# The block-to-block step of an S5 scan by doubling instead of one block after the other

## The chip, the cores and the metric

The kernel runs on one core of one Trainium2 chip. The metric is the device time of one execution in microseconds, as the median of several runs. The chip's engines are named as in the profile: PE is TensorE (PEld its weight loads), DVE is VectorE, ACT is ScalarE, POOL is GpSimd and SP is SyncE, which only issues transfers here.

## What is computed

One inference step of a decoder trunk of two layers, for 1024 prompt rows and 8 x 8 sample rows that share the weights (1088 rows of 1024 features). Layer 0 has two mixers side by side behind one input projection: an S5 state space (32 groups of 16 channels, 64 complex states each) and a gated DeltaNet (GDN, 4 heads). Layer 1 is an RWKV-7 mixer. Each layer ends with a SwiGLU feed-forward part. The change is in S5. What matters of the reference there:

```python
bu = einsum("gpc,blgc->blgp", bb, uf)
bu[:, 0] += ab * h0
x[t] = ab * x[t - 1] + bu[t]
y = real(einsum("gcp,blgp->blgc", c, x)) + d_skip * uf
```

All of `ab`, `bu`, `x` and `c` are complex and are held as a real and an imaginary part; the recurrence runs over the 1024 prompt rows, and for the samples over 8 rows each.

## The kernel before, in words

**Rows, chunks, blocks.** S5 cuts time into chunks of 8 rows: 128 chunks for the prompt and one for each of the 8 sample sequences. Inside a chunk the work is matrix products; from chunk to chunk the state is carried by a scan. The tile `Z` (128 partitions x 2 x 16 x 136) holds, for 16 state columns, the real and the imaginary part of the state before each chunk. A chunk's step multiplies by `a` to the power 8, where `a` is `ab` above.

**Constants** (`S5.consts`, L580). Small VectorE instructions on 128x16 work out `a` and its powers: `pw` holds powers 0 to 8, `p8` (L671) holds the powers 0 to 8 of `a` to the 8th, each by a complex multiplication `cmul` (L650, six instructions). `p8s` (L681) is a copy of the imaginary parts, once with the sign turned. The planner places these among the work that prepares the input rows.

**Adding up** (`S5.adds`, L760). For each of four groups `m` of four state columns the input part of every chunk is computed on TensorE and copied into `Z`.

**The scan** (`S5.scan`, L786). It is called twice, once for groups 0 and 1 and once for groups 2 and 3, each time on 8 state columns. All of it is VectorE work. A step (L793 to L800) adds to a part `o` of `Z` a power times a part `x` of `Z`, as four instructions: two multiplications into `m1` and `m2`, their sum, and the addition to `o`. The 128 chunks stand as 16 blocks of 8. First each block is scanned by itself: 7 steps on all 16 blocks at once (256 columns, L802). Then the last chunk of each block is carried to the last chunk of the next one: 15 steps, each on one block (16 columns, L804). Then each block's carried state is added to the first seven chunks of the next one: 7 steps on 15 blocks (240 columns, L806), which do not depend on each other. GpSimd then copies the final state and the sample states, and a last step advances the samples.

**Outputs** (`S5.outputs`, L819). Per group, TensorE multiplies `Z` (L840) and the inputs (L838) by weights made in `weights` (L717), and ScalarE and VectorE apply a GELU (L842 to L845).

**The order of the work.** Behind S5 in the program stand the input projections of the GDN (`qkvz`, L1806, products `pi` of L322) and the GDN segments, whose tiles take the room that S5 leaves. The framework's planner orders the instructions of every engine's queue by a simulated time line (L2112); nothing in S5 fixes an order by hand. So the projections are spread among the S5 products on TensorE. Each queue is worked through in its order on the chip.

Of the kernel before, what the change touches and what calls it, by code (L numbers as in the profile page):

```python
# [8 lines left out]
F32 = mybir.dt.float32  # L9
# [559 lines left out]
class S5:  # L569
# [10 lines left out]
    def consts(self, after, lam_re, lam_im, log_step, b_re, b_im, c_re, c_im, dskip, h0):  # L580
        K, nc, cp = self.K, self.K.nc, self.cp
        v = nc.vector
# [3 lines left out]
        def col(name, n=16):  # L586
            return cp.tile([128, n], F32, name=name)
# [32 lines left out]
        z = col("zz")  # L620
# [29 lines left out]
        def cmul(o, a, b, e, tag):  # L650

            (orr, oi), (ar, ai), (br, bi), sh = o, a, b, list(o[0].shape)
            tl = lambda: (self.wp or cp).tile(sh, F32, tag=tag, name=tag)
            t = tl()
            e.tensor_mul(orr, ar, br)
            e.tensor_mul(t, ai, bi)
            e.tensor_sub(orr, orr, t)
            t = tl()
            e.tensor_mul(oi, ar, bi)
            e.tensor_mul(t, ai, br)  # L660
            e.tensor_add(oi, oi, t)
# [6 lines left out]
        b4 = lambda i: pw[:, i, 4:5, :].to_broadcast([128, 4, 16])  # L668
        cmul((pw[:, 0, 5:9], pw[:, 1, 5:9]), (pw[:, 0, 1:5], pw[:, 1, 1:5]), (b4(0), b4(1)), v, "cm4")

        p8 = cp.tile([128, 2, 9, 16], F32, name="p8")  # L671
        self.p8 = p8
        v.tensor_copy(p8[:, :, 0:1], pw[:, :, 0:1])
        v.tensor_copy(p8[:, :, 1:2], pw[:, :, 8:9])
        Q = lambda j: (p8[:, 0, j], p8[:, 1, j])
# [2 lines left out]
        cmul(Q(4), Q(2), Q(2), v, "cm")  # L678
        b8 = lambda i: p8[:, i, 4:5, :].to_broadcast([128, 4, 16])
        cmul((p8[:, 0, 5:9], p8[:, 1, 5:9]), (p8[:, 0, 1:5], p8[:, 1, 1:5]), (b8(0), b8(1)), v, "cm4")  # L680
        p8s = self.p8s = cp.tile([128, 2, 9, 16], F32, name="p8s")  # L681
        v.tensor_scalar(p8s[:, 0], p8[:, 1], -1.0, None, op0=OP.mult)
        v.tensor_copy(p8s[:, 1], p8[:, 1])

# [101 lines left out]
    def scan(self, fin, qs):  # L786

        nc, wp, Z, SV = self.K.nc, self.wp, self.Z, self.SV
        v = nc.vector
        nq = qs.stop - qs.start  # L790
        z = Z[:, :, qs, 1:129].rearrange("p i q (b j) -> p i q b j", j=8)

        def step(o, x, j, n):  # L793

            m1 = wp.tile([128, 2, nq, 16], F32, tag="m1", name="m1")[:, :, :, :n]
            m2 = wp.tile([128, 2, nq, 16], F32, tag="m2", name="m2")[:, :, :, :n]
            v.tensor_mul(m1, x, self.p8[:, 0, j, qs][:, None, :, None].to_broadcast([128, 2, nq, n]))
            v.tensor_mul(m2, x[:, 1::-1], self.p8s[:, :, j, qs][:, :, :, None].to_broadcast([128, 2, nq, n]))
            v.tensor_add(m1, m1, m2)
            v.tensor_add(o, o, m1)  # L800

        for j in range(1, 8):  # L802
            step(z[:, :, :, :, j], z[:, :, :, :, j - 1], 1, 16)
        for b in range(1, 16):  # L804
            step(z[:, :, :, b:b + 1, 7], z[:, :, :, b - 1:b, 7], 8, 1)
        for j in range(7):  # L806
            step(z[:, :, :, 1:16, j], z[:, :, :, 0:15, 7], j + 1, 15)

        nc.gpsimd.tensor_copy(fin[:, :, qs, 0:1], Z[:, :, qs, 128:129])
        nc.gpsimd.tensor_copy(Z[:, :, qs, 128:136], self.h0[:, :, qs])  # L810
        step(SV[:, :, qs], Z[:, :, qs, 128:136], 1, 8)
        nc.gpsimd.tensor_copy(fin[:, :, qs, 1:9], SV[:, :, qs])
# [1303 lines left out]
```

## Time and profile before

| | |
|---|---|
| median of 3 runs | 3686.85 us |
| the runs | 3677.34, 3686.85, 3695.24 us |
| the profiled execution, its own time | 3692.78 us |
| its span from first to last instruction | 3691.0 us |
| mean granted TensorE clock | 0.951 |
| first `Z` input copied / last scan instruction starts | 122.9 us / 253.5 us |
| S5 output products of `Z` (L840) | 194.3 to 279.2 us |

The page's slices of the span, from which the stages can be read (each of the 40 digits is the busy share, in tenths, of 92.3 us; S5 lies in slices 2 to 4):

```profile
PE   7889999999997899999999988899999999999998
...
DVE  7976888754448556766666573577778887553444
...
PEclk8989987999998899999999999999999999999999
```

A duration in a timeline is that of one instruction; the next one of the same engine may start a little before the end of it, so the length of a run of instructions is taken from starts. "Idle before" in square brackets is the time for which the engine stood still before the instruction, with what released it.

### The profile page before, as it was taken

The page shows a single profiled execution, that of the slowest core. Times are in us where ns is not written, and L with a number is a line of the kernel's source. Part 1 is how long each engine was busy: PE and PEld are TensorE (multiplying, and loading weights), DVE is VectorE, ACT ScalarE, POOL GpSimd, SP SyncE. Part 2 cuts the span into 40 slices and gives each one's busy share as a digit, 9 for nine tenths or more (in the row PEclk, how much of TensorE's full clock was granted, in tenths as well). Part 3 has the DMA queues.
Part 4 walks back from the last instruction along what each step waited for, and adds up shares of the span by engine and source line. Part 5 has one row for each costly group of instructions (what it writes and reads, how often), then busy time and mean ns, then how long its engine had stood idle before and what let it go on. Part 6 is the DMA issues. An engine that isn't in the chain of part 4 may idle for free.

```text
span 3691.0 us, 77399 instructions
## 1 busy us (share of the span) xinstructions
PE 3429.1 (93%) x29894; PEld 3191.9 (86%) x29894; DVE 2393.1 (65%) x6834; ACT 1389.0 (38%) x3264; POOL 1047.3 (28%) x1037
## 2 busy tenths in 40 slices
PE   7889999999997899999999988899999999999998
PEld 6879888989997788899999888888888888899997
DVE  7976888754448556766666573577778887553444
ACT  3333333322224444444444354433343443222222
POOL 3322133223316551211110052334333332132221
PEclk8989987999998899999999999999999999999999
DMA  3434453345553584344444446732223322422322
GB/s 102 99 85 127 98 170 101 129 141 183 187 178 124 185 288 148 111 139 143 138 138 128 144 142 215 246 108 81 79 83 87 96 82 88 159 75 74 93 80 67
DMA packets 387552, 474.36 MB, mean 129 GB/s; under 512 B 142312, under 2 KB 305896, under 8 KB 387184
## 3 DMA queue, kind: packets, MB, share of 16 engines
q1 hardware_dynamic: 364144, 447.13, 39.7%
q10 hardware_dynamic: 23040, 22.29, 1.8%
q8 instruction: 235, 3.85, 0.4%
q14 instruction: 133, 1.09, 0.1%
HBM read 344.32 MB, written 123.79 MB: 127 GB/s over the span
## 4 chain that ended last, share of the span: by engine, by line
PE 64%; DVE 21%; DMA 9%; issue 3%; ACT 2%; POOL 1%; SPq 1%; DVEq 0%; ACTq 0%; POOLq 0%
PE pg L322 24%; PE pd L322 11%; PE pj L322 5%; PE po L322 5%; PE pi L322 3%; DVE T L188 2%; DVE Tm L186 2%; PE pg L1649 2%; DMA raw<-in_wd 1%; DVE mx L1350 1%; DMA rkb<-dks 1%; PE pc L1689 1%; PE py L1698 1%; DMA Tc<-dT 1%; DMA dT<-T 1%
## 5 line engine op out<-in xcount | busy, mean ns | idle before, releaser
L322 PE MATMUL pg<-hi,wh 128*128 128x288 f32 (+1 forms) x2816 | 833.1, 296 | 15.7 <-DVE s L511 9.5
L322 PE MATMUL pg<-lo,wh 128*128 128x288 f32 (+1 forms) x2816 | 833.4, 296 | 6.9 <-DVE lo L409 5.6
L322 PE MATMUL pg<-hi,wl 128*128 128x288 f32 (+1 forms) x2816 | 828.6, 294 | 1.0 <-POOL wl L309 1.0
L309 POOL TENSOR_TENSOR wl<-raw,wh 128x1024 fp32r<-128x1024 f32 (+3 forms) x205 | 482.5, 2355 | 897.9 <-ACT wh L305 842.9
L322 PEld LDWEIGHTS pg<-hi,wh 128*128 128x128 f32 x2816 | 539.4, 192 | 24.0 <-DVE s L511 11.2
L322 PEld LDWEIGHTS pg<-lo,wh 128*128 128x128 f32 x2816 | 539.7, 192 | 13.8 <-DVE lo L409 7.5
L322 PEld LDWEIGHTS pg<-hi,wl 128*128 128x128 f32 x2816 | 539.3, 192 | 5.1 <-POOL wl L309 1.4
L305 ACT CAST wh<-raw 128x1024 fp32r<-128x1024 f32 (+3 forms) x309 | 313.2, 1014 | 363.6 <-PE pg L322 102.9
L322 PE MATMUL pd<-ah,wdh 128*128 128x256 f32 (+1 forms) x1280 | 386.0, 302 | 9.3 <-DVE x L534 6.0
L322 PE MATMUL pd<-ah,wdl 128*128 128x256 f32 (+1 forms) x1280 | 372.8, 291 | 0.3 <-DMA wdl<-low_wd 0.3
L322 PE MATMUL pd<-al,wdh 128*128 128x256 f32 (+1 forms) x1280 | 371.0, 290 | 0.0
L322 PEld LDWEIGHTS pd<-ah,wdh 128*128 128x128 f32 x1280 | 242.5, 189 | 21.4 <-DVE x L534 9.1
L322 PE MATMUL pj<-hi,wh 128*128 128x256 f32 (+1 forms) x768 | 233.3, 307 | 16.1 <-ACT st L1405 7.3
L322 PEld LDWEIGHTS pd<-ah,wdl 128*128 128x128 f32 x1280 | 242.7, 190 | 3.3 <-issue 1.6
L322 PEld LDWEIGHTS pd<-al,wdh 128*128 128x128 f32 x1280 | 243.0, 190 | 1.9 <-issue 1.6
L322 PE MATMUL pj<-lo,wh 128*128 128x256 f32 (+1 forms) x768 | 234.4, 307 | 9.5 <-DVE lo L409 8.2
L322 PE MATMUL pj<-hi,wl 128*128 128x256 f32 (+1 forms) x768 | 231.2, 305 | 10.9 <-DMA wl<-low_wr 7.0
L534 DVE TENSOR_TENSOR x<-x,pd 128x256 f32<-128x256 f32 (+1 forms) x384 | 162.5, 426 | 91.0 <-PE pd L322 87.6
L305 ACT CAST wdh<-raw 128x384 fp32r<-128x384 f32 (+1 forms) x224 | 111.2, 496 | 248.0 <-PE pd L322 158.8
L322 PE MATMUL pi<-hi,wh 128*128 128x272 f32 x640 | 192.2, 300 | 1.5 <-ACT pr L1809 1.3
L322 PE MATMUL pi<-lo,wh 128*128 128x272 f32 x640 | 191.2, 299 | 0.0
L322 PE MATMUL pi<-hi,wl 128*128 128x272 f32 x640 | 190.8, 298 | 0.0
(643 smaller groups left out, 8059.3 us busy)
## 6 DMA issues: line engine op xcount, KB each, us to landing
raw<-in_wg SPq DMA_DIRECT2D x88, 512.0 KB
raw<-in_wup SPq DMA_DIRECT2D x88, 512.0 KB
raw<-in_wd SPq DMA_DIRECT2D x192, 192.0 KB
low_wg<-wl SPq DMA_DIRECT2D x22, 512.0 KB
low_wup<-wl SPq DMA_DIRECT2D x22, 512.0 KB
wl<-low_wg SPq DMA_DIRECT2D x22, 512.0 KB
wl<-low_wup SPq DMA_DIRECT2D x22, 512.0 KB
raw<-in_win SPq DMA_DIRECT2D x20, 512.0 KB
```

Source lines behind the costliest of these rows:

```text
L186: v.tensor_mul(mm, L[:nl, j:j + 1, j + 1:16].to_broadcast([nl, j + 1, n]), T[:nl, 0:j + 1, j:j + 1].to_broadcast([nl, j + 1, n]))
L188: v.tensor_tensor(T[:nl, 0:j + 1, j + 1:16], T[:nl, 0:j + 1, j + 1:16], mm, op=op)
L305: nc.scalar.copy(wh, raw)
L309: (lo or nc.gpsimd).tensor_sub(wl, raw, wh)
L322: self.nc.tensor.matmul(ps, a[k], b[:, c:c + cn], start=i == 0, stop=i == last)
L534: v.tensor_add(x[m][:, c:c + cn], x[m][:, c:c + cn], ps)
L1350: v.scalar_tensor_tensor(t, xx[k][:, c:c + cn], self.vec[:, j, k:k + 1], x[k][:, c:c + cn], op0=OP.mult, op1=OP.add)
L1649: nc.tensor.matmul(pgs[hl][:, i], bk[R, c0 + i], rhs, start=True, stop=True)
L1689: nc.tensor.matmul(two(pb), two(BG[:, u, 0]), U, start=True, stop=True)
L1698: nc.tensor.matmul(o, BG[:, u, 1, hl], XV[:, u, hl], start=False, stop=True)
```

## The change

The 15 steps of L804 are replaced by four. Step `i` adds, to the last chunk of every block from block `d` on, the power times the last chunk of the block `d` before it, for `d` = 1, 2, 4 and 8; it works on 16 - `d` blocks at once. For this the powers 16, 32 and 64 of `a` to the 8th are needed besides power 8. They are worked out by three more squarings in the constants, and `p8` and `p8s` grow from 9 to 12 entries.

```diff
--- before.py
+++ after.py
@@ -668,7 +668,7 @@
         b4 = lambda i: pw[:, i, 4:5, :].to_broadcast([128, 4, 16])
         cmul((pw[:, 0, 5:9], pw[:, 1, 5:9]), (pw[:, 0, 1:5], pw[:, 1, 1:5]), (b4(0), b4(1)), v, "cm4")
 
-        p8 = cp.tile([128, 2, 9, 16], F32, name="p8")
+        p8 = cp.tile([128, 2, 12, 16], F32, name="p8")
         self.p8 = p8
         v.tensor_copy(p8[:, :, 0:1], pw[:, :, 0:1])
         v.tensor_copy(p8[:, :, 1:2], pw[:, :, 8:9])
@@ -678,7 +678,10 @@
         cmul(Q(4), Q(2), Q(2), v, "cm")
         b8 = lambda i: p8[:, i, 4:5, :].to_broadcast([128, 4, 16])
         cmul((p8[:, 0, 5:9], p8[:, 1, 5:9]), (p8[:, 0, 1:5], p8[:, 1, 1:5]), (b8(0), b8(1)), v, "cm4")
-        p8s = self.p8s = cp.tile([128, 2, 9, 16], F32, name="p8s")
+
+        for j in range(9, 12):
+            cmul(Q(j), Q(j - 1), Q(j - 1), v, "cm")
+        p8s = self.p8s = cp.tile([128, 2, 12, 16], F32, name="p8s")
         v.tensor_scalar(p8s[:, 0], p8[:, 1], -1.0, None, op0=OP.mult)
         v.tensor_copy(p8s[:, 1], p8[:, 1])
 
@@ -801,8 +804,10 @@
 
         for j in range(1, 8):
             step(z[:, :, :, :, j], z[:, :, :, :, j - 1], 1, 16)
-        for b in range(1, 16):
-            step(z[:, :, :, b:b + 1, 7], z[:, :, :, b - 1:b, 7], 8, 1)
+
+        for i in range(4):
+            d = 1 << i
+            step(z[:, :, :, d:16, 7], z[:, :, :, 0:16 - d, 7], 8 + i, 16 - d)
         for j in range(7):
             step(z[:, :, :, 1:16, j], z[:, :, :, 0:15, 7], j + 1, 15)
```

## Rows read from the trace of the kernel before

**Rows 1.** The page, busy time and share of the span by engine.
```profile
PE 3429.1 (93%) x29894; PEld 3191.9 (86%) x29894; DVE 2393.1 (65%) x6834; ACT 1389.0 (38%) x3264; POOL 1047.3 (28%) x1037
```

**Rows 2.** Busy time by stretch: start:end, length, engines (instructions), clock, DMA share, GB/s.
```profile
300.00:350.00 50.00, 48.35 (x386) 47.93 (x385) 36.09 (x83) 16.17 (x30) 10.78 (x10) 1.00 0.41 125
450.00:460.00 10.00, 4.51 (x51) 3.90 (x48) 9.36 (x30) 6.20 (x17) 1.70 (x2) 0.50 1.03 232
```

**Rows 3.** The chain that ended last, 119 to 254 us, shares by line.
```profile
by line: DVE Z L800 21.3%; DVE m L799 20.6%; DVE m L797 16.8%; DVE m L798 14.6%; DMA U<-du 5.4%; issue 4.3%; DVE ca L659 2.1%; DVE cb L660 2.0%; DVE ga L843 1.8%; DVE es L737 1.8%; DVE ba L655 1.6%; PE pv L781 1.6%; DVE ba L659 1.5%; ACT w 
```

**Rows 4.** Timeline of TensorE, the two stops for the scan (in brackets).
```profile
194.29 1.24 PE L840 MATMUL py<-Z,w 64*128 64x136 f32 x4 [9.60 <-DVE Z L800]
...
252.89 1.24 PE L840 MATMUL py<-Z,w 64*128 64x136 f32 x4 [5.62 <-DVE Z L800]
```

**Rows 5.** Timeline of VectorE, narrow steps of scan one: start, length, engine, line, instruction.
```profile
160.35 0.17 DVE L797 TENSOR_TENSOR m<-Z,p 128x16 f32<-128x16 f32 x1
...
160.64 2.42 DVE L799 TENSOR_TENSOR m<-m,m 128x16 f32<-128x16 f32 x1
...
163.32 0.19 DVE L797 TENSOR_TENSOR m<-Z,p 128x16 f32<-128x16 f32 x1
...
173.85 0.59 DVE L798 TENSOR_TENSOR m<-Z,p8s 128x240 f32<-128x240 f32 x1
```

**Rows 6.** Busy time in the block of narrow steps of scan two.
```profile
218.16:235.74 17.58, 17.58 (x139) 17.12 (x140) 16.28 (x67) 7.70 (x14) 6.55 (x5) 1.00 0.41 111
```

**Rows 7.** VectorE's groups in that block: other work than the steps.
```profile
L845 DVE SCALAR_TENSOR_TENSOR yg<-ga,py 128x272 f32<-128x272 f32 x4 | 1.7, 431 | 0.0
L737 DVE TENSOR_TENSOR es<-es,dd 32x64 f32<-32x64 f32 x1 | 1.2, 1245 | 0.0
L843 DVE SCALAR_TENSOR_TENSOR ga<-ga,py 128x272 f32<-128x272 f32 x2 | 0.9, 434 | 0.0
```

**Rows 8.** Timeline of VectorE, one step of the first loop and its successor.
```profile
137.05 0.63 DVE L797 TENSOR_TENSOR m<-Z,p 128x256 f32<-128x256 f32 x1
...
138.24 0.42 DVE L799 TENSOR_TENSOR m<-m,m 128x256 f32<-128x256 f32 x1
...
139.26 0.74 DVE L655 TENSOR_TENSOR ca<-cre,pw 128x576 f32<-128x576 f32 x1
```

**Rows 9.** Timelines of GpSimd and VectorE, one instruction each.
```profile
211.77 2.35 POOL L309 TENSOR_TENSOR wl<-raw,wh 128x1024 fp32r<-128x1024 f32 x1 [1.85 <-ACT wh L305]
...
211.86 2.54 DVE L799 TENSOR_TENSOR m<-m,m 128x256 f32<-128x256 f32 x1
```

**Rows 10.** VectorE's groups by shape, 100 to 260 us: the steps on 256 columns.
```profile
L800 DVE TENSOR_TENSOR Z<-Z,m 128x256 f32<-128x256 f32 x14 | 12.1, 863 | 0.2
L798 DVE TENSOR_TENSOR m<-Z,p8s 128x256 f32<-128x256 f32 x14 | 10.7, 764 | 0.0
...
L799 DVE TENSOR_TENSOR m<-m,m 128x256 f32<-128x256 f32 x14 | 9.9, 710 | 0.3
L797 DVE TENSOR_TENSOR m<-Z,p 128x256 f32<-128x256 f32 x14 | 9.5, 676 | 0.2
```

**Rows 11.** Timeline of VectorE behind the constants.
```profile
88.73 0.28 DVE L912 TENSOR_SCALAR gs<-gs,dtb 64x128 f32<-64x128 f32 x1 [9.38 <-DMA gs<-dgs]
```

**Rows 12.** Busy time by stretch, the clock after TensorE's stops.
```profile
170.00:175.00 5.00, 2.63 (x22) 2.41 (x20) 4.45 (x24) 2.19 (x2) 0.94 (x3) 1.00 0.33 112
187.00:188.00 1.00, 0.00 (x0) 0.00 (x0) 0.96 (x3) 0.00 (x0) 0.00 (x0) 0.50 0.00 0
252.00:253.00 1.00, 0.11 (x1) 0.14 (x1) 0.97 (x4) 0.00 (x0) 0.00 (x0) 0.50 0.00 0
```

**Rows 13.** The chain that ended last, behind the second stop, in order of time.
```profile
261.98 8.96 PE pi L322 x57
270.94 0.23 PE py L838 x2
...
279.44 26.41 PE pi L322 x209
```

## The prediction

> **What bounds the kernel now.** I first read the busy shares: TensorE works 93% of the span [rows 1], so a change in VectorE work counts only where TensorE waits for it. Then the busy time by stretch: while the GDN segments and the input projections run side by side, TensorE has next to no room (48.35 of 50 us), and at 450 to 460 us, when the projections have run out, there is a hole, 4.51 of 10 us busy at half the clock [rows 2]. Third, the chain that ended last, cut to 119 to 254 us, where S5 runs: its four largest shares are all the scan's own lines, L797 to L800, 73% together [rows 3]. So in S5 the end is set by VectorE, one instruction after another, while TensorE fills its time with projections. Last, TensorE's timeline: it stops for the scan twice, 9.60 us before the first output product of group 0 (end of scan one) and 5.62 us before that of group 2 (end of scan two) [rows 4]. A shorter scan can take from these two stops and, by starting GDN sooner, from the hole at 450.
>
> **What the change removes.** Each of the two scans has 15 narrow steps of four instructions on 128x16 (8 state columns, real and imaginary). They run one behind the other: each needs the result before it. Scan one's block goes from 160.35 to 173.85, 13.50 us, with one instruction of 2.42 us in the first step; the other 14 take 173.85 - 163.32 = 10.53 us, 0.752 us a step [rows 5]. Undisturbed, 15 steps are 11.28 us. Scan two's block takes 17.58 us [rows 6], of which 1.7 + 1.2 + 0.9 = 3.8 us is other work put between [rows 7], so 13.8 us.
>
> **What it adds.** Four steps per scan, on n = 15, 14, 12 and 8 blocks, that is 240, 224, 192 and 128 columns, still one behind the other and with the same stride (every eighth element of Z). The nearest row is a dependent step of the first loop, 256 columns, same stride: 139.26 - 137.05 = 2.21 us [rows 8]. A straight line through 16 columns (0.75) and 256 (2.21) is 6.08 ns a column: 2.11 + 2.02 + 1.82 + 1.43 = 7.38 us. Saved per scan 11.28 - 7.38 = 3.9 us, for both **7.8 us** of VectorE on the chain. Fewer instructions, but 784 columns instead of 240: that is why 60 instructions becoming 16 gives a third and not three quarters.
>
> [...]
>
> **Bounds of the saving.** Some VectorE instructions get long while GpSimd works: the L799 at 211.86 took 2.54 us while GpSimd's L309 ran from 211.77 for 2.35 us [rows 9]; the same line on as many columns is 0.42 us elsewhere [rows 8]. If wide steps meet such holds as often as the 14 of 256 columns did, a step costs the sum of the group means, 676 + 764 + 710 + 863 = 3.01 us [rows 10], four cost 12.05, and each scan loses 0.8 us against 11.28: -1.5 us for both. If instead the holds inside today's blocks go too, the saving is 13.50 + 13.8 - 2 x 7.38 = 12.5 us. I take 7.8: GpSimd has the same work before and after, so a hold that leaves one step meets the next.
>
> **The constants.** Three complex multiplications, 18 instructions on 128x16, are added behind the powers. At 0.19 us (a narrow L797 [rows 5]) they are 3.4 us, and p8s becomes a third longer. They come at the end of the constants, which the scan alone reads; behind these VectorE is idle for 9.38 us up to 88.73, waiting for the DMA of the gate rows [rows 11], and the first block that reads the new ones begins at 160.35 [rows 5]. That hole hides them: I put 0. Were they sorted between the instructions that prepare the last chunk for TensorE, they would cost up to 3.4 us. No DMA and no queue is touched.
>
> **What arrives at the end.** If TensorE's order stays, its first stop shrinks from 9.60 to 5.7 us. Then it comes to the second stop 3.9 us sooner and Z is there 7.8 us sooner: 5.62 becomes 1.7 us. So the whole 7.8 us passes to TensorE, whose full stretch at 300 to 350 hands it on. What is late next is TensorE itself. And the clock: in both stops the granted clock falls to half (0.50 at 187 and at 252), while a stop of 2.37 us inside 170 to 175 left it at 1.00 [rows 12]. At 1.7 us the second fall should not come. Its price: outputs of group 2 from 252.89 to 261.98, 9.09 us, against 279.44 - 270.94 = 8.50 for group 3; then 57 projection products in 8.96 us, 0.157 each, against 26.41 / 209 = 0.126 later [rows 4, 13]: 0.6 + 1.8 = **2.4 us**. The first fall stays, since 5.7 us is near the 5.62 that halved it.
>
> Sum: 7.8 + 2.4 = 10.2 us. The profiled execution took 3692.8 us (3691.0 of span), and would take 3682.6; it stands 5.9 us above the median of 3686.85. From the median: **3676.7 us**, -0.28%. A measurement of this kernel can tell about 0.5% from no change, 18.4 us: the forecast is "same".
>
> **Rivals.**
> A. The order moves along. The order on all engines comes from a planner; if it books the scan 3.9 us shorter, it puts the output products that much earlier in TensorE's queue, both stops stay and no time is won there. What is won is the earlier start of GDN, and that pays only where TensorE has a hole, 5.5 us at 450 to 460 [rows 2]: 3681.4 us. For it: the queue is written anew. Against: the two stops show that plan and chip differ here anyway.
> B. The wide steps are held by GpSimd as the other wide ones are: +1.5 us, 3688.4 us. For it: the group means. Against: inside today's blocks GpSimd worked 6.55 us in 17.58 [rows 6], and such holds cost the narrow steps too. [...]
> C. Slower. The planner books no holds and takes a wide step for little more than a narrow one, so it expects 11.28 - 4 x 0.75 = 8.3 us less per scan and moves the output products up by that, while the chip holds the wide steps as in B. Each stop grows by 8.3 + 0.8 = 9.1 us, TensorE stands 18.2 us longer and nothing later takes it back: 3705.1 us. It decides as soon as the booked saving is over the real one; at 3.9 us real it is 4.4 per stop, 8.8 in all. For it: both stops today are of this kind, TensorE there too early. Against: no row shows what the planner books, and in the second block TensorE was full all 17.58 us [rows 6], so the plan had work enough to put there.
> D. More than the forecast: the holds go with the narrow steps (12.5 us), and with stops of 3.5 us and none both clock falls go (2 x 2.4): 17.3 us, 3669.5 us. Against: GpSimd's work has to go somewhere.
> That the change does nothing is hardly possible: the narrow steps are gone from the program, and the wide ones have rows.
>
> **Chances.** Forecast 0.42, A 0.20, B 0.13, C 0.10, D 0.15. Runs of before scatter from 3677.34 to 3695.24, so each case carries some 9 us to both sides. Range: down to D less that scatter, 3660, up to B with it and into the lower part of C, 3700; what is left out is most of C and the tails. Faster by over 0.5% (below 3668.4): half of D and a fifth of the forecast, 0.16. Slower by over 0.5% (above 3705.3): half of C and a tail of B, 0.07. Within: 0.77.
>
> **What would show it.** Right: 16 instructions of L797 to L800 in place of 60 per scan, blocks of 7 to 8 us; TensorE's stops of 6 and below 2 us, the second over at some 245 instead of 252.89 us; clock at 1.00 behind the second; the last projection 8 to 10 us sooner. Wrong: blocks of 11 us or more (B), stops longer than 9.6 and 5.6 (C), stops unchanged with a smaller hole at 450 (A). A difference that arises only behind 450 us, in work that the diff does not touch, would mean that the new order of the queues decides and not the scan.

## The result, and the profile after

The changed kernel is **slower** by half a per cent: 3714.51 us (median of 7 runs, 3704.57 to 3723.56) against 3691.18 us of the kernel before on the same chip (7 runs, 3677.34 to 3702.74). The ratio is 1.0052, with a 95% interval from 1.0035 to 1.0069. The forecast was 3676.7 us with a range of 3660 to 3700. The two medians alone give 1.0063; the text goes by the ratio on record with its interval.

The profiled execution has a span of 3706.3 us, 15.3 more than before. The page has the same work in it, 70 VectorE instructions fewer (it answers to [rows 1]):

```profile
PE 3428.2 (92%) x29894; PEld 3187.4 (86%) x29894; DVE 2386.1 (64%) x6764; ACT 1392.3 (38%) x3264; POOL 1047.4 (28%) x1037
```

**The scan did get shorter.** VectorE's timeline shows the first instruction of each of the four wide steps of scan one and of what follows (start, length, engine, line, instruction; the lines of the step now begin at L800):

```profile
157.79 0.67 DVE L800 TENSOR_TENSOR m<-Z,p 128x240 f32<-128x240 f32 x1
...
160.21 0.56 DVE L800 TENSOR_TENSOR m<-Z,p 128x224 f32<-128x224 f32 x1
...
162.28 0.49 DVE L800 TENSOR_TENSOR m<-Z,p 128x192 f32<-128x192 f32 x1
...
164.21 0.40 DVE L800 TENSOR_TENSOR m<-Z,p 128x128 f32<-128x128 f32 x1
...
165.72 0.60 DVE L800 TENSOR_TENSOR m<-Z,p 128x240 f32<-128x240 f32 x1
```

The block takes 165.72 - 157.79 = 7.93 us (steps of 2.42, 2.07, 1.93 and 1.51) where it took 13.50 [rows 5]. In scan two it is 10.35 us (209.43 to 219.78) instead of 17.58 [rows 6]. The last scan instruction starts at 241.09 instead of 253.49 us.

**What TensorE waited for** is the second thing to see. This is the view of waits of TensorE from 150 to 300 us (what waited and on what: us in all, times, the longest), first of the kernel before:

```profile
PE py L840 <- DVE Z L800: 15.2, 2, 9.6
PE py L838 <- ACT w2p L827: 2.4, 1, 2.4
PE pi L322 <- ACT pr L1809: 1.3, 1, 1.3
```

and then of the changed kernel (`w2p` is now L832, `pr` L1814):

```profile
PE py L845 <- DVE Z L803: 6.8, 1, 6.8
PE pi L322 <- ACT pr L1814: 5.1, 2, 3.0
PE py L843 <- ACT w2p L832: 4.2, 3, 2.8
```

The wait for the scan fell from 15.2 to 6.8 us; the waits for the weights (`w2p`) and for the copies of the projections' results (`pr`, of `pi`) grew from 3.7 to 9.3. In sum 18.9 became 16.1.

**Where the time was lost** shows in TensorE's timeline. In the kernel before, the weights' products `e` of group 3 stand ahead of group 2's outputs, and GDN's first product (`pq`) is issued at 305.68:

```profile
240.25 1.93 PE L733 MATMUL e<-ca,bd 128*32 128x128 f32 x16
...
305.68 0.95 PE L972 MATMUL pq<-one,sq 128*128 128x1 f32 x8
```

In the changed kernel they stand behind them, run at half the clock (0.50 granted from 259.54 to 263.09 us, 1.00 from 240.25 to 242.12 before), and `pq` comes at 318.11, 12.4 us later:

```profile
182.52 1.24 PE L845 MATMUL py<-Z,w 64*128 64x136 f32 x4 [6.84 <-DVE Z L803]
...
243.91 0.82 PE L843 MATMUL py<-U,w2p 128*128 128x136 f32 x2 [2.76 <-ACT w2p L832]
...
259.54 3.62 PE L736 MATMUL e<-ca,bd 128*32 128x128 f32 x16
...
290.26 0.73 PE L845 MATMUL py<-Z,w 64*128 64x136 f32 x4
...
318.11 0.95 PE L977 MATMUL pq<-one,sq 128*128 128x1 f32 x8
```

From then on little changes: `pq` + 3385.3 us is the end of the span before, `pq` + 3388.2 after. So the loss lies ahead of 318 us, and it is TensorE's. What stands in its queue from the first adding-up product `pv` to `pq` can be counted by the view of busy time by stretch (start:end, length; busy us and instructions of TensorE, its weight loads, VectorE, ScalarE, GpSimd; granted clock; DMA), once for all instructions and once for those of the projections `pi` alone. The kernel before:

```profile
119.24:305.68 186.44, 164.84 (x1214) 151.98 (x1215) 148.61 (x312) 67.28 (x136) 51.74 (x43) 0.90 0.36 99
...
119.24:305.68 186.44, 110.15 (x806) 106.89 (x806) 0.00 (x0) 13.15 (x34) 0.00 (x0) 0.90 0.36 99
```

The changed kernel:

```profile
116.61:318.11 201.50, 182.64 (x1294) 166.89 (x1295) 142.05 (x224) 69.89 (x140) 54.55 (x44) 0.89 0.35 98
...
116.61:318.11 201.50, 120.30 (x885) 116.83 (x885) 0.00 (x0) 14.20 (x37) 0.00 (x0) 0.89 0.35 98
```

Read it as a sum. The stretch grew by 201.50 - 186.44 = 15.06 us: 10.15 by 885 instead of 806 projection products put ahead of GDN, 7.65 by the other products (S5's own, 62.34 against 54.69 us), and -2.74 by less idle time. VectorE's work went down by 6.6 us and counted nowhere. Those 79 products are not extra work, they are only done sooner; the projections end at 431 us instead of 447 and are missing as a filler later, while GDN starts late.

Of the 7.65 us, 1.7 are group 3's `e`, which run at half the clock (3.62 us at 0.50 instead of 1.93 at 1.00). Some 5.5 are group 2's outputs: all 48 products take 259.54 - 243.91 = 15.63 us, where before 40 took 9.09 [rows 4, 13] and 8 had stood ahead of the stop with 1.02 us. For the 40 the clock is no difference, both kernels run them at half of it (0.50 from 252.89 to 261.98 us before, 0.50 from 243.91 to 259.54 in the changed kernel). Their order is. In the kernel before, eight products of `Z` stand in a run, in the changed kernel four, and eight take 256.02 - 254.81 = 1.21 us, four 245.86 - 244.66 = 1.20. So the 32 products of `Z` take 6.0 us in five runs before and 9.6 in eight runs after. The other 1.9 us are the inputs' products, above all the eight that had run ahead of the stop (239.23 to 240.25 us, in one run and at a clock of 1.00) and now come in pairs at 0.50; order and clock can't be told apart there. The kernel before:

```profile
254.81 1.29 PE L840 MATMUL py<-Z,w 64*128 64x136 f32 x8
256.02 0.82 PE L838 MATMUL py<-U,w2p 128*128 128x136 f32 x2
```

The changed kernel:

```profile
244.66 1.27 PE L845 MATMUL py<-Z,w 64*128 64x136 f32 x4
245.86 0.82 PE L843 MATMUL py<-U,w2p 128*128 128x136 f32 x2
```

The order itself is no guess: this is TensorE's queue behind group 0's weights in both programs (`pi` projections, `py` S5 outputs, `e` weights' products, with their numbers as the program writes them; the trace shows each `py` and `e` as two; `pq` is GDN's).

```
before  pi148 py4 e8 pi59 py20 pi42  py24 e8 pi144 py4 e8 pi39 py20 pi57 py24 pi209 pq
after   pi148 py4 e8 pi7  py20 pi102 py24 e8 pi153 py24 e8 pi151 py24 pi216 pq
```

Nothing in the diff says that; the planner wrote every queue anew. That it did so because it books the scan as shorter is likely, but no row shows it.

### The profile page after: what moved, and what is told of

Same layout as the page of the kernel before. It is cut to its first block, busy times and chain, and to the rows that moved or that the text cites. A ratio compares the mean times of both kernels' runs of the same rounds, so it can differ in the third digit from the quotient of the medians.

```text
span 3706.3 us, 77309 instructions
## 1 busy us (share of the span) xinstructions
PE 3428.2 (92%) x29894; PEld 3187.4 (86%) x29894; DVE 2386.1 (64%) x6764; ACT 1392.3 (38%) x3264; POOL 1047.4 (28%) x1037
## 4 chain that ended last, share of the span: by engine, by line
PE 60%; DVE 24%; DMA 9%; issue 3%; ACT 2%; SPq 1%; POOL 1%; ACTq 0%; DVEq 0%; POOLq 0%
PE pg L322 23%; PE pd L322 11%; PE pj L322 5%; PE po L322 4%; PE pi L322 3%; DVE T L188 2%; DVE Tm L186 2%; PE pg L1654 1%; DMA raw<-in_wd 1%; DVE mx L1355 1%; DMA Tc<-dT 1%; DMA dT<-T 1%; PE py L1703 1%; DMA rkb<-dks 1%; PE pc L1694 1%
## 5 line engine op out<-in xcount | busy, mean ns | idle before, releaser
L322 PE MATMUL pg<-hi,wh 128*128 128x288 f32 (+1 forms) x2816 | 833.5, 296 | 13.8 <-DVE s L511 8.5
L322 PE MATMUL pg<-lo,wh 128*128 128x288 f32 (+1 forms) x2816 | 832.1, 296 | 10.3 <-DVE lo L409 9.4
L309 POOL TENSOR_TENSOR wl<-raw,wh 128x1024 fp32r<-128x1024 f32 (+3 forms) x205 | 482.3, 2354 | 911.3 <-ACT wh L305 807.1
```

The lines of the kernel that those rows point to most:

```text
L309: (lo or nc.gpsimd).tensor_sub(wl, raw, wh)
L322: self.nc.tensor.matmul(ps, a[k], b[:, c:c + cn], start=i == 0, stop=i == last)
```

## The experiments

Two theories were held against each other from the start. **The order theory**: the doubling itself costs nothing, the queues written anew do. **The rival**: the wide steps (or the constants) cost the time by themselves.

**e1, one edge in the kernel before.** The narrow scan, but group 3's weights' products queued behind group 2's last output product:

```diff
+                with K.tc.issue_after(self.last.ins) if m == 3 else ExitStack():
                     nc.tensor.matmul(e[:, q], ...
```

> The kernel before, with its 15 narrow steps and without the new powers; one thing is changed: the products that begin the weights of group 3 (L733, 16 of them) are queued on TensorE behind the last output product of group 2, as they stand in the changed kernel. Theory 1 (the weights' chain of the last group, begun too late, puts off the end of S5 and with it the start of GDN): the last output product of S5 moves from 279 to some 290 us, the first GDN inverse product (L216) from 356 to 368 us or later, and the time grows by 10 to 25 us, ratio to before 1.003 to 1.007. Theory 2 (the wide steps or the new order behind 450 us cost the time, each for itself): no change beyond 0.2%, since the scan and all else are as before.

Measured: 1.0077 [1.0052, 1.0102]. TensorE's timeline has the same pattern as the changed kernel: the products at half the clock behind group 2 (0.50 from 261.00 to 265.19 us), and a late `pq`:

```profile
261.86 3.62 PE L734 MATMUL e<-ca,bd 128*32 128x128 f32 x16
...
319.64 0.95 PE L973 MATMUL pq<-one,sq 128*128 128x1 f32 x8
```

The ratio is a little above the range that the order theory had. The planner filled the gap with projections here too, 915 ahead of `pq`. The first feed-forward product comes 17.6 us late, in the changed kernel 15.7. The slowness of the change is had without its scan. This kernel loses as much again later, behind 1080 us, where its queues also came out differently.

**e2, only the constants.** The three more powers with the narrow scan.

> The three more powers and the larger p8 and p8s alone, the scan with its 15 narrow steps as before. Theory 1: same as before within 0.2%, the 18 instructions lie in VectorE's idle time behind the constants, S5's last output product at 279 us. Theory 2, if the constants are the cost: the rows of the first projection products move by 3 us and the time grows by 3 us or more.

Measured: 1.0007 [0.9991, 1.0022], with TensorE's queue the same as before from end to end. The constants are free, as forecast.

**e3 and e4, all weights one group ahead**, once with the doubling and once with the narrow scan:

```diff
-        w2, w3 = self.weights(m)
+        w2, w3 = self.next if m else self.weights(m)
         nc.scalar.copy(w2p, w2.rearrange("p g (t c) -> p g c t", c=16))
+        if m < 3:
+            self.next = self.weights(m + 1)
```

> The changed kernel (doubling), with the weights of group m+1 traced before the output products of group m instead of behind them. Theory 1: the chain of the weights no longer stands behind the outputs; the last output product of S5 comes at 265 us or sooner (279 before, 291 changed), GDN starts sooner, and the time falls below that of before, by 5 to 25 us, ratio 0.993 to 0.999. Theory 2 (the wide steps or the order behind 450 us by itself): as slow as the changed kernel, ratio 1.003 to 1.007.

> The kernel before with its 15 narrow steps, weights of group m+1 traced ahead as in the run before. It tells what of that run is the doubling and what the weights. Theory 1: with the weights out of the way the scan alone sets the end of S5, so this one ends S5 8 to 12 us behind the doubling with weights ahead, and is slower than it by 5 to 12 us; against before 0 to 10 us faster. Theory 2: the two differ by nothing that follows the end of S5.

Measured: 1.0044 [1.0026, 1.0061] and 1.0030 [1.0016, 1.0045]. In e3 only 681 projections stand ahead of `pq`, which comes at 289.51, and the first feed-forward product is 17.7 us sooner than before; yet the last GDN inverse product comes at 808.5 instead of 787.6 us, 20.9 late. A start that is sooner does not have to end sooner. By the ratio e3 is a miss for the order theory and lies in the rival's range; but e4 loses too, without any wide step, and was not slower than e3, as the order theory had it. These two runs do not part the theories.

**e5, the doubling with TensorE's old order.** Edges without any wait hold TensorE's queue in S5 to that of the kernel before, but for group 3's `e`, which come just ahead of group 2's first `u` instead of just behind them: S5's products behind the projection that stood before them, the next projection behind the last of these S5 products (`u` and `y` are the output products of the inputs and of `Z`, `e` those of the weights, each with its group; the numbers count projections). For this group 3's weights are written ahead of group 2's outputs. Behind S5 all queues then come out as before. VectorE's queue in S5 is not held, and the planner wrote it anew.

```diff
+        for n, k in ((763, "u0"), (763, "e1"), (822, "y0"), (864, "u1"), (864, "y1"), (864, "e2"),
+                     (1008, "u2"), (1008, "e3"), (1047, "y2"), (1104, "u3"), (1104, "y3")):
+            for ins in self.held[k]:
+                self.tc.add_manual_dep(ins.ins, self.pis[n - 1].ins.name, ...NoSync...)
```

> The doubling scan, with TensorE's queue held to that of the kernel before through S5 (the same 489 projection products in the same places, group 3's weight products ahead of group 2's outputs); behind S5 every queue comes out as in the kernel before. It is the case for which the forecast's sum was made ('if TensorE's order stays'). Forecast and order theory: the last scan ends some 12 us sooner than before, the last S5 output product some 8 to 11 us sooner (268 to 271 us instead of 279.2), the first GDN inverse product at 345 to 348 instead of 355.6, and the ratio to before is 0.996 to 0.999. Rival, the doubling itself costs the time (wide steps that hold something up): S5's end as late as in the changed kernel, some 290, ratio 1.004 to 1.006.

Measured: **0.9999** [0.9982, 1.0016]. The rival is refuted: with TensorE's order kept, the doubling costs nothing. But it gains nothing either, against the forecast. The view by stretch from `pv` to `pq`, and the view of waits from 150 to 300 us:

```profile
115.34:301.52 186.18, 162.24 (x1214) 148.80 (x1215) 142.30 (x225) 67.11 (x136) 53.58 (x43) 0.90 0.36 100
...
115.34:301.52 186.18, 106.70 (x806) 103.49 (x806) 0.00 (x0) 13.16 (x34) 0.00 (x0) 0.90 0.36 100
```

```profile
PE py L864 <- ACT w2p L851: 17.6, 2, 16.6
PE pi L338 <- ACT pr L1836: 2.9, 1, 2.9
PE py L867 <- DVE Z L822: 0.7, 1, 0.7
```

The stretch is 186.18 us long against 186.44: 0.3 us gained. TensorE works 2.60 us less in it and stands 2.34 us longer. The wait for the scan is all but gone, 0.7 instead of 15.2 us, and a wait for the weights stands in its place, 17.6 instead of 2.4. Two timeline rows tell which, the copy on ScalarE and TensorE's stop:

```profile
206.85 1.95 ACT L851 COPY w2p<-w 128x1024 f32<-128x1024 f32 x1
```

```profile
208.85 0.82 PE L864 MATMUL py<-U,w2p 128*128 128x136 f32 x2 [16.65 <-ACT w2p L851]
```

In the kernel before, group 1's weights were copied at the very same time, and just in time:

```profile
206.85 2.06 ACT L827 COPY w2p<-w 128x1024 f32<-128x1024 f32 x1
```

```profile
210.57 0.39 PE L838 MATMUL py<-U,w2p 128*128 128x136 f32 x2
```

The copy ends at 208.91 and its reader starts at 210.57: 1.66 us to spare. In e5 the weights came no sooner, though scan one and group 0's outputs did. On ScalarE the copy stands behind the GELU of group 0, whose VectorE part stands in turn between the steps of scan two, and that place is new. Scan two begins, and the first GELU instruction follows, in e5 at

```profile
182.56 0.61 DVE L820 TENSOR_TENSOR m<-Z,p8s 128x256 f32<-128x256 f32 x1
...
201.42 0.43 DVE L870 SCALAR_TENSOR_TENSOR ga<-ga,py 128x272 f32<-128x272 f32 x1
```

and in the kernel before at

```profile
195.10 0.60 DVE L798 TENSOR_TENSOR m<-Z,p8s 128x256 f32<-128x256 f32 x1
...
200.81 0.43 DVE L843 SCALAR_TENSOR_TENSOR ga<-ga,py 128x272 f32<-128x272 f32 x1
```

In e5 it stands behind 20 instructions of scan two, in the kernel before behind 7 (in the changed kernel behind 10). ScalarE, ready with its part at 183.9 us, waits for it:

```profile
201.89 0.43 ACT L871 ACTIVATE ga<-ga 128x272 f32<-128x272 f32 x1 [7.63 <-DVE ga L870]
```

So e5 tells what the doubling costs with TensorE's old order, nothing. What it gains with all orders kept, VectorE's too, no run shows.

**e6, the counterpart**: the narrow scan with S5's part of TensorE's queue as in the changed kernel (same kind of edges).

> The counterpart: the narrow scan of the kernel before, with TensorE's queue through S5 held to that of the changed kernel (561 projection products ahead of S5's end, group 3's weight products behind group 2's outputs). Order theory: as slow as the changed kernel or slower; the scans end some 12 us later than there and TensorE's first stop grows from 6.84 us to some 15, the last S5 output product comes at 293 to 300 us, the ratio to before is 1.005 to 1.010. Rival, the doubling itself costs the time: no slower than before, ratio 0.998 to 1.002, S5's end near 279.

Measured: 1.0102 [1.0082, 1.0122], just above the upper end of the order theory's range. The stretch to `pq` and the first stop for the scan:

```profile
117.45:323.30 205.85, 180.35 (x1293) 165.62 (x1294) 149.41 (x313) 69.60 (x140) 55.55 (x44) 0.88 0.33 95
```

```profile
192.58 0.79 PE L861 MATMUL py<-Z,w 64*128 64x136 f32 x2 [13.77 <-DVE Z L820]
```

The order costs with the narrow scan as well. TensorE's queue is the changed kernel's up to 450 us and like neither kernel's from there on, so the ratio has that in it too.

**e7, doubling in scan one alone**, nothing held.

```diff
+        if qs.start == 0:
+            for i in range(4):
...
+        else:
             for b in range(1, 16):
```

> Only scan one by doubling, scan two narrow as before; nothing is held. The planner again puts group 3's weight products behind group 2's outputs, and 554 projection products ahead of S5's end instead of 489. Forecast's terms: half of the saving, ratio 0.998 to 1.000. Order theory: the last S5 output product at 287 to 292 us like the changed kernel's 290.7, the first GDN inverse product some 15 us later than before, ratio 1.003 to 1.007.

Measured: 1.0091 [1.0066, 1.0117], more than either theory had; `pq` at 318.77, with 873 projections ahead of it and group 3's weights behind group 2's outputs as in the changed kernel. Half of the change turns the order as the whole does.

**e8, the changed kernel with group 3's weights alone ahead** (the edit of e3, for `m == 2` only).

> The changed kernel with the weights of group 3 alone written ahead of group 2's output products; 441 projection products come to stand ahead of S5's end. If the start of GDN decides the total: last S5 output product at 262 to 270 us, first GDN inverse product at 342 to 348 (before 355.6), ratio 0.995 to 0.999. If an order of the later work that comes out differently takes the gain back, as in the version with all weights ahead (there 17.7 us sooner at the first feed-forward product, 11.3 us later at the end): the same times up to 360 us, ratio 1.002 to 1.006.

Measured: 1.0068 [1.0041, 1.0094]. S5 ends 3.4 us sooner than before, `pq` comes at 302.94 (763 projections) and the first feed-forward product 1.9 us late; but the last GDN inverse product is 25.5 us late. Turning this one edge back repairs what lies ahead of 611 us, and the later queues, new once more, lose it again, a little more than the second theory had.

**e9 to e12: which part of the order.** A table of the order in which one kernel's queues hold all instructions traced behind S5 is laid on another kernel, as edges without waits on all five engines:

```diff
+    for engine, text in LATER.items():
...
+                    tc.add_manual_dep(mine[k], mine[last].name, ...NoSync...)
```

> The changed kernel, with its own scan and its own order in S5 (561 projection products ahead of S5's end, group 3's weight products behind group 2's outputs), but with the order of every queue behind S5 taken from the kernel before: 137 instead of 216 projection products stand between S5's end and GDN's first product. Theory 'S5's own order': S5's last output product at 288 to 293 us and GDN's first inverse product not before 368 (before 355.6, changed kernel 372.7), ratio 1.004 to 1.006 as in the changed kernel. Theory 'the order behind S5': S5's end is as late, but GDN's first inverse product comes at 350 to 357 us, and the ratio is 0.997 to 1.001.

> The kernel before, narrow scan and its own order in S5, with the order of every queue behind S5 taken from the changed kernel: 288 instead of 209 projection products between S5's end and GDN's first product. Theory 'the order behind S5': S5's last output product at 279 us as before, GDN's first inverse product some 10 us later than before (363 to 368), ratio 1.003 to 1.007. Theory 'S5's own order': GDN's first inverse product within 3 us of 355.6, ratio 0.998 to 1.002.

Measured: e9 1.0056 [1.0037, 1.0074], e10 1.0061 [1.0048, 1.0074]. Each theory of these two runs was right in one and wrong in the other: S5's new order alone is enough to lose the half per cent, and so is the order behind it. They do not add up to more. The stretches from `pv` to `pq` say why. e9:

```profile
116.69:318.40 201.71, 177.53 (x1215) 160.08 (x1215) 138.68 (x223) 66.84 (x135) 52.76 (x43) 0.87 0.32 89
...
116.69:318.40 201.71, 112.43 (x806) 108.08 (x806) 0.00 (x0) 12.58 (x33) 0.00 (x0) 0.87 0.32 89
```

and e10:

```profile
118.32:315.48 197.16, 175.99 (x1293) 163.38 (x1294) 149.01 (x312) 69.74 (x140) 54.16 (x44) 0.90 0.36 99
...
118.32:315.48 197.16, 121.61 (x885) 118.39 (x885) 0.00 (x0) 14.31 (x37) 0.00 (x0) 0.90 0.36 99
```

e10 has 885 projections, and they make 11.5 us more, of which idle time and other products take back 0.4 and 0.3: the stretch is 10.7 us longer than before. Behind `pq` its profiled execution, the slowest of its six, loses 14.3 us more, which this does not explain. e9 has the old 806, but its S5 products took 65.10 us instead of 54.69 (group 2's outputs stand as in the changed kernel and take 15.30 us, and the granted clock is 0.87 instead of 0.90), the projections took 2.3 us more, and the idle time is 2.6 us longer. So the loss up to `pq` has two sources: filler put ahead of GDN, and S5 products that take longer by their order and by the clock.

> The changed kernel with group 3's weights ahead of group 2's outputs (1.0068 by itself, last S5 output at 275.8 us), with the order of every queue behind S5 taken from the kernel before. If the newly written later order took 1.0068, it falls to 0.996 to 1.000, with every milestone behind 355 us 2 to 8 us sooner than before. If something in S5 took it, it stays above 1.004.

> The version with the doubling scan and all weights one group ahead (1.0044 by itself, last S5 output at 262.4 us, then 20 us lost between 594 and 810 us), with the order of every queue behind S5 taken from the kernel before: 339 projection products between S5's end and GDN's first product. The candidate for the fastest. If only the later order cost it the gain: ratio 0.995 to 0.999. Otherwise 1.002 to 1.006, with the loss again between 594 and 810 us.

Measured: e11 (e8 with the old later order) 1.0045 [1.0032, 1.0059], e12 (e3 with it) 1.0038 [1.0020, 1.0055]. Both miss the return to before that their first theory had: better than e8, and about as e3. The ratios lie where the second theories put them, but e12's loss does not: its last GDN inverse product comes at 790.1 us, 2.5 late. With 806 projections to do ahead of `pq`, neither starts GDN sooner (308.17 and 307.44 us), although S5 ends 3.6 and 14.6 us sooner.

**e13 and e14**: e3 and e8 again, the old order laid on only from GDN's second half and the feed-forward part on.

> The version with the doubling scan and all weights one group ahead (1.0044 by itself), its own order in S5 and in the first half of GDN, but from GDN's second half and the feed-forward part on every queue in the order of the kernel before. By itself it was 17.7 us ahead at the first feed-forward product and 11.3 us behind at the end. If the later order that came out differently took the gain: ahead by 10 to 17 us at the first feed-forward product, and still by 8 to 17 us at the end, ratio 0.995 to 0.998, faster than both kernels. If something else took it (the work itself late for another engine): again behind at the last GDN inverse product (790 us or later, before 787.6), ratio 1.002 to 1.006.

> The changed kernel with group 3's weights ahead of group 2's outputs (1.0068 by itself; 1.9 us behind before at the first feed-forward product, 25.5 us at the last GDN inverse product), from GDN's second half and the feed-forward part on in the order of the kernel before. If the later order took the time: within 4 us of before at every milestone from 611 us on, ratio 0.998 to 1.002. If something else took it: 10 us or more behind at the last GDN inverse product, ratio above 1.004.

Measured: 1.0090 [1.0071, 1.0109] and 1.0102 [1.0082, 1.0122]: misses for the first theory of both. The second had the last GDN inverse product late, as it is (812.4 and 819.4 us, before 787.6), with a smaller ratio in e13. In e13 the loss comes at the seam, before the point where it was looked for: the first feed-forward product is 20 us late, while e3 had it 17.7 us early. It looks as if an order that was written for one start does not fit another; no run shows that by itself.

All kernels in one table: projections ahead of `pq`, its start, and the rest of the span behind it, in us.

| kernel | scan | S5 order | later order | `pi` | `pq` | rest | ratio |
|---|---|---|---|---|---|---|---|
| before | narrow | old | old | 806 | 305.7 | 3385.3 | 1 |
| e2 | narrow | old | old | 806 | 304.8 | 3394.9 | 1.0007 |
| e5 | wide | old | old | 806 | 301.5 | 3386.2 | 0.9999 |
| changed | wide | new | new | 885 | 318.1 | 3388.2 | 1.0052 |
| e9 | wide | new | old | 806 | 318.4 | 3392.5 | 1.0056 |
| e10 | narrow | old | new | 885 | 315.5 | 3399.6 | 1.0061 |
| e11 | wide | e8's | old | 806 | 308.2 | 3387.5 | 1.0045 |
| e12 | wide | e3's | old | 806 | 307.4 | 3389.2 | 1.0038 |
| e7 | wide, narrow | own | own | 873 | 318.8 | 3394.9 | 1.0091 |
| e1 | narrow | one edge | own | 915 | 319.6 | 3407.9 | 1.0077 |
| e6 | narrow | new | own | 885 | 323.3 | 3407.7 | 1.0102 |
| e4 | narrow | own | own | 789 | 303.1 | 3402.1 | 1.0030 |
| e3 | wide | own | own | 681 | 289.5 | 3412.8 | 1.0044 |
| e8 | wide | own | own | 763 | 302.9 | 3417.6 | 1.0068 |
| e13 | wide | e3's | own, then old | 681 | 289.0 | 3429.7 | 1.0090 |
| e14 | wide | e8's | own, then old | 763 | 303.9 | 3423.0 | 1.0102 |

`pq` and rest are of one execution each. The first `pv` alone lies between 115.2 and 119.2 us in them, and e2, whose TensorE queue is that of the kernel before, has a rest 9.6 us longer; so differences of under 10 us between rows say nothing. Two things stand above that. With the old or the changed kernel's later order the rest is 3385 to 3400 us, whatever the scan; where the later queues came out otherwise it is mostly 3402 to 3430. The rest also holds the projections that are still to be done: 125 more in e3 and e13 than in the kernel before, an estimated 16 us at 0.126 each [rows 13]. And no order that was tried beats that of the kernel before.

**What stays open**: where e11 and e12 lose their 0.4%. Their profiled executions are within 6 us of the profiled one of before and cannot show it: e11's (3697.5 us) is the fastest of its six, with a median of 3704.5, while that of before (3692.8) stands above the 3687.9 of the runs that e11 and e12 were compared with. Open too is why the other later orders cost 15 to 45 us behind `pq`: between 305 and 1100 us TensorE's longest wait for VectorE is 5.2 us in e3 and e13 and 4.1 in e8. That it is the order, and not the work, is shown by e5, e6, e9 and e10 only for the orders of the two kernels.

## Why the prediction was wrong

**What bounds the kernel: half right.** S5's end was set by VectorE, as the chain said [rows 3]. But the kernel's end does not follow S5's end: in e12 S5 ends 14.6 us sooner and nothing is won. The changed kernel lost by what TensorE's queue holds ahead of GDN's first product, and by how long that takes; and a sooner first product is not enough either, as e3 shows. The forecast treated the projections as a filler that adapts. They are fixed in a queue: in the kernel before, TensorE stood for 9.60 us ahead of group 0's first product of `Z` [rows 4] in the middle of a projection's 24 products; six were issued up to 184.40 us, the other 18, of the same weight tile, from 203.31, behind that group's outputs.

**What is removed and added: right, a little small.** The narrow block without a hold was put at 11.28 us; e6 has 11.24 in scan one. The wide one was put at 7.38; it is 7.93, from rows of a wide step [rows 8], and 7.94 in e5. The two blocks of the kernel before took 13.50 + 13.8 us without the other work in them, those of the changed one 7.93 + 9.05 (10.35 less 1.3 for three GELU instructions): 10.3 us less, between the 7.8 of the forecast and the 12.5 of D. As the prediction said, the holds did not go with the narrow steps: scan two has one of 2.58 us in the block, and that of scan one now stands just behind it, 2.74 us at 167.30. Beside both, GpSimd ran an L309, for 2.67 us from 211.74 and for 2.60 us from 166.90.

**The constants: right.** e2 puts them at nothing that can be told.

**The step that failed is "What arrives at the end"**, twice. It begins "If TensorE's order stays", and the order did not stay: 79 more projections stand ahead of `pq` and group 3's `e` behind group 2's outputs, and GDN starts 12.4 us later. In e5 TensorE's order stays, and there the next sentence falls: "So the whole 7.8 us passes to TensorE ... What is late next is TensorE itself." Late next were group 1's weights, which had 1.66 us to spare before and were 16.65 us late in e5. The wait for the scan shrank even more than forecast (15.2 to 0.7 us, forecast 15.2 to 7.4), and 0.3 us arrived. TensorE's order was too narrow a condition: the weights were late by the place of the GELU in VectorE's queue, which is new in e5 as well.

**The clock: the term came, mis-sized, and was paid back.** In e5 the second fall is gone (1.00 from 251.10 to 262.73 us), and the same 40 products of group 2's outputs take 259.34 - 254.30 = 5.04 us instead of 9.09:

```profile
254.30 0.73 PE L867 MATMUL py<-Z,w 64*128 64x136 f32 x4
...
259.34 0.40 PE L338 MATMUL pi<-hi,wh 128*128 128x272 f32 x1
```

That is 4.05 us, where the prediction put 0.6: it set 9.09 beside group 3's 8.50, but those are more products, 48 at a clock of 1.00, in the slower order. What was won so was lost on group 1's outputs, which in e5 run at half the clock behind the stop of 16.65 us (15.63 us, at 0.50 from 208.43 to 223.94, instead of 8.59 in the kernel before, at 1.00 from 210.5 to 219). In the changed kernel the second fall came with another stop, 2.76 us for group 2's weights, and this stretch follows:

```profile
250.00:260.00 10.00, 10.00 (x33) 7.42 (x34) 1.75 (x4) 1.95 (x5) 0.00 (x0) 0.50 0.00 0
```

**The rivals.** A had the order move along, and took that for harmless: it still won 5.5 us in the hole at 450. C named the planner and its time, 3705.1 us, is that of the changed kernel (1.0052 x 3686.85 = 3706.0), but by another mechanism: it wanted longer stops for the scan, and they fell from 15.2 to 6.8 us. A chance of 0.10 for any order that loses was too low; the forecast of what a planner writes had no row to stand on, and it should have been given more weight on both sides. B is refuted by the blocks of 7.93 and 10.35 us.

**The sign to look for** ("a difference that arises only behind 450 us ... would mean that the new order of the queues decides") pointed at the right cause and the wrong place: 12.4 us are there at 318.

## What to carry to other kernels

Ahead of shortening the last operand of a wait, read in the trace when the other operands of the same instruction and of the next ones came, and what they hang on: in e5, 14.5 us less of waiting for the scan turned into 15.2 us more of waiting for the weights. Where a planner writes the queues, a change of one engine's work is also a change of all orders; hold the old order with edges that cost no wait to measure the two apart, on every engine that matters and not on TensorE alone, and count what stands ahead of the next stage's first product. A filler that is done sooner is not time won if the stage behind it starts later: the changed kernel's projections ended at 431 instead of 447 us, with GDN 12.4 us late.

## What was not expected of the hardware

**The length of a stop did not tell whether TensorE's clock fell.** Ahead of group 0's `e` TensorE stops for 2.69 us (to 144.71) in the kernel before and for 2.70 us (to 140.77) in e5. Behind it the granted clock was 0.51 of full speed from 146 to 149 us in the one, and 1.00 from 142 to 145 us in the other:

```profile
146.00:149.00 3.00, 3.00 (x16) 3.00 (x15) 2.96 (x5) 2.10 (x2) 1.50 (x1) 0.51 0.00 0
```

```profile
142.00:145.00 3.00, 3.00 (x26) 2.85 (x25) 2.97 (x5) 2.06 (x2) 1.54 (x1) 1.00 0.00 0
```

In the changed kernel a stop of 2.14 us was followed by 0.50, while one of 2.37 us in the kernel before (to 174.02) left the clock at 1.00 up to 175 us [rows 12]:

```profile
201.46 0.39 PE L322 MATMUL pi<-hi,wh 128*128 128x272 f32 x1 [2.14 <-ACT pr L1814]
```

```profile
203.00:205.00 2.00, 2.00 (x11) 2.00 (x10) 1.90 (x4) 1.85 (x2) 0.00 (x0) 0.50 0.86 258
```

So one row was too little ground for the prediction's step from 2.37 to 1.7 us. How long the low clock lasted differed as well: behind the stop of 2.97 us (to 163.43) projections followed and the clock was 0.50 from 165 to 168 and 1.00 again from 169 us; behind that of 2.76 us S5's outputs followed and it was 0.50 from 245 to 263.

**Eight products took the time of four.** Products of `Z` (64*128 in the trace, where those of the inputs are 128*128) took 1.21 us in a run of eight and 1.20 in a run of four, both at a clock of 0.50. In e5, at 1.00, a run of eight took 256.06 - 255.39 = 0.67 us and one of four 254.96 - 254.30 = 0.66. In the changed kernel's order, without runs of eight, the same 32 products of group 2 took 9.6 us at 0.50 instead of 6.0.
